# A hybrid decoder block on one core: first attention blocks and first FFN blocks planned ahead, GpSimd's block subtractions split up

## The chip, the cores and the metric

One core of one Trainium2 chip runs the whole layer in one launch. The metric is the device time of that core in microseconds, the median of the runs shown. TensorE (PE) does matrix products and transposes, VectorE (DVE), ScalarE (ACT) and GpSimd (POOL) the rest; SyncE (SP) issues all transfers in order.

## The reference

One layer over 2048 tokens of width 1024, all in float32:

```python
h = rmsnorm(x, g_mix);  p = h @ w_in                        # 1024 -> 2560
y_a = conformer_conv(a_val, a_gate, ...)                    # GLU, causal conv of 31, LayerNorm, swish
y_b = chunked_sgu(b_u, b_v, ...)                            # gelu, LayerNorm, 128x128 mixing per chunk
# stick-breaking attention, 8 heads of 64, 128-query blocks over the causal keys:
z = q @ k.T * d**-0.5;  mask = s_pos < t_pos
log_1m_beta = where(mask, -softplus(z), 0);  log_beta = -softplus(-z)
a = where(mask, exp(log_beta + reverse_cumsum(log_1m_beta) - log_1m_beta), 0);  o = a @ v
x = x + (concat(_rms(y_a), _rms(y_b), _rms(y_c)) * g_out) @ w_out
h = rmsnorm(x, g_ffn);  up = causal_dwconv(h @ w_up)        # 1024 -> 2 x 2816, conv of 3
x = x + (silu(gate) * val) @ w_down;  return rmsnorm(x, g_final)
```

## The kernel before, in words

Every float32 product is three TensorE products of rounded parts (`mm3`, L114: high by high, high by low, low by high); the low part of an operand is its float32 value less the rounded one.

**Projections** (L437 to L514), two halves of 1024 tokens. Key parts `kh_d`, `kl_d`, query parts, values `v_d` and the two other branches' outputs go to DRAM. The convolution runs on VectorE, a step at a time between projection blocks. PSUM has eight banks: `tp` (x transposes) and `cvp` (convolution) lie on the left, `bt` (branch transposes, `pst`) and `pj` (three projection blocks) on the right. The last value blocks leave PSUM through `vs` (L499).

**Attention** (L879 to L923): 320 steps of one 128-query block by up to 512 keys of one head. Four steps are a unit (one head and key chunk), two units (both heads) a chunk of a pair of heads; a query stretch of 512 has four pairs. In a step `front` (L715) makes the scores `pz` (L732, L735), ACT their sigmoids `om` (L737), VectorE the running product (scan, L740 on the diagonal, L745 elsewhere); six steps later `transpose_a` (L752) transposes `om` into `pat` (L758) and splits it into `ah` and `al`; `al` is made by VectorE (L770) for even blocks and by GpSimd (L767) for odd ones; eight steps later `times_v` adds the products with V in `po` (L779, L780). `finish_pair` (L782) brings `po` out as `ych`. `load_kv` fetches keys and values for pairs after the first into `kv`; for the first pair (`pre`, L541) they are in the x tiles' buffers (`xi`).

**Work let in between.** Output projections are generators (`out_proj`, L646; g=0 branches A and B, g=1 the attention's part) whose matmuls are let in behind the score product of a step (`tc.issue_after`), 1.8 stops a step up to step 32, 0.65 behind. After g=1 a row block of 128 tokens is normed into `h` (L682 to L694) and, two row blocks at a time, `store_blocks` (L615) writes seven blocks of `h` to `hc_d`: three as they are, four as differences, made by GpSimd, and by VectorE for the last query stretch. These are the operands of a seven-product scheme for a 2x2 block product, which the FFN uses. `down_blocks` (L598), called every 20 steps from step 40, does the same for w_down: two loads (`wd0`, `wd1`, one buffer each), four subtractions on GpSimd (L607 to L610), four stores.

**Border.** The last out_proj (query stretch 3, g=1) runs with `up_weights(0)` (L959) between; `stage_first` has put the first four blocks of `h` on the chip. `h_blocks` (L1015) transposes a block into `pth` (L1026), casts it (`thh`, L1031) and subtracts (`thl`, L1032). The tiles for these lie where the last out_proj's weights were; their PSUM banks (`ups`) where `atp` and `otp` were.

**FFN** (L1156 on): seven products for each pair of channel blocks (`prod`), then the down product (`pd`).

**What orders the work.** The program is traced in the order of the code, and a planner gives each engine its order ahead of the run: by a simulated time line it takes, of the instructions whose inputs and buffers are ready, the one traced first; `tc.high_priority(offset=n)` counts an instruction as traced n earlier. Each engine then works strictly in that order. A tile waits only for the tiles that had its bytes before (`reuse_waits="tile"`).

Of the kernel before, what the change touches and what calls it, by code (L numbers as in the profile page):

```python
# [15 lines left out]
P = 128  # L16
# [4 lines left out]
def kernel(  # L21
# [114 lines left out]
    xp = pool(cl, "xp", 4)  # L136
    tp = pool(cl, "tp", 2, space=PSUM)
    cvp = pool(cl, "cvp", 1, space=PSUM)
    hp = pool(cr, "hp", 2, "right")
    wp = pool(cr, "wp", 5, "right")  # L140
    rp = pool(cr, "rp", 2, "right")
# [294 lines left out]

    for hf in range(2):  # L437
# [31 lines left out]
        for c0, hd, ld in ((1536, kh_d, kl_d), (1024, qh_d, ql_d)):  # L469
            w = load_w(c0)  # L470
            for ct in range(NPAIR):
# [43 lines left out]
    def load_q(tiles, qs, pr):  # L515
        qA, qB = tiles
        t_s = slice(qs * 512, (qs + 1) * 512)
        dma32(qA[0:64], qh_d[pr, 0:64, t_s])
        dma32(qA[64:128], ql_d[pr, 0:64, t_s])
        dma32(qB[0:64], ql_d[pr, 64:128, t_s])  # L520
        dma32(qB[64:128], qh_d[pr, 64:128, t_s])
        return tiles

    def load_kv(tiles, kc, pr):
        kA, kB, lA, lB, vv = tiles
        k_s = slice(kc * 512, (kc + 1) * 512)
        for hd, th_, tl_ in ((0, kA, lA), (1, kB, lB)):
            hr = slice(64 * hd, 64 * hd + 64)
            for r in (slice(0, 64), slice(64, 128)):
                dma32(th_[r], kh_d[pr, hr, k_s])  # L530
                dma32(tl_[r], kl_d[pr, hr, k_s])
        dma32(
            vv,
            v_d[kc * 4 : kc * 4 + 4, :, pr * 256 : (pr + 1) * 256].rearrange(
                "n p c -> p n c"
            ),
        )
        return tiles


    pre = [  # L541
        xp.tile([P, D], F32R, tag="xi", name=f"pre{i}").rearrange("p (a c) -> p a c", a=2)
        for i in range(4)
    ]
    first_q = load_q((pre[0][:, 0, :], pre[0][:, 1, :]), 0, 0)
    first_kv = load_kv(
        (
            pre[1][:, 0, :], pre[1][:, 1, :], pre[2][:, 0, :], pre[2][:, 1, :],
            pre[3].rearrange("p a (n c) -> p (a n) c", c=256),
        ),  # L550
        0, 0,
    )
    while later:
# [5 lines left out]
    kv = pool(cr, "kv", 2, "right")  # L559
    ap_ = pool(cr, "ap", 1, "right")  # L560
    tp2 = pool(cr, "tp2", 3, "right")
    co = ExitStack()
    opp = pool(co, "opp", 2, "right", space=PSUM)
    zp = pool(cr, "zp", 2, "right", space=PSUM)
    cl.close()
    cl = ExitStack()
    wo = pool(cl, "wo", 1)
# [3 lines left out]
    atp = pool(cl, "atp", 2, space=PSUM)  # L571
    otp = pool(cl, "otp", 2, space=PSUM)
# [3 lines left out]
    G.memset(mask[:, : 512 - P], 0.0)  # L576
    G.memset(mask[:, 512 - P :], 1.0)
    G.affine_select(
        out=mask[:, 512 - P :], in_=mask[:, 512 - P :], pattern=[[1, P]],
        compare_op=ALU.is_ge, fill=0.0, base=0, channel_multiplier=-1,  # L580
    )
# [64 lines left out]
    def out_proj(qs, g, kept=()):  # L646
# [6 lines left out]
        for j in range(4):  # L653
            n = qs * 4 + j
            x1, (yh, yl) = nxt, ys.pop(0)
            for nh in range(2):
# [58 lines left out]
    def front(p, kc, hd, j):  # L715
# [20 lines left out]
        om = ap_.tile([P, 512], F32, tag="om", name="om", bufs=13)[:, :w_]  # L736
# [15 lines left out]
    def transpose_a(p, kc, hd, b, a4):  # L752
# [10 lines left out]
        if b % 2:  # L763
# [3 lines left out]
            G.tensor_tensor(al[:, c_], ar[:, c_], ah[:, c_], op=ALU.subtract)  # L767
# [541 lines left out]
```

## Time and profile before

| | us |
|---|---|
| median of 3 runs (2558.9 to 2566.23) | 2563.68 |
| the profiled execution | 2561.74 |
| its span, first to last instruction | 2559.7 |
| TensorE busy | 2408.8 (94%) |
| VectorE busy | 1852.8 (72%) |
| ACT busy | 1202.3 (47%) |
| GpSimd busy | 1215.6 (47%) |

The mean granted clock of TensorE is 0.976 of full speed. In the views a name such as `al` is the tile written, "<-" the tiles read, L767 the line; "[7.52 <-ACT vs L499]" says that the engine was idle 7.52 us before, until that instruction. SPq is the queue of SP.

### The profile page before, as it was taken

What the parts mean: (1) busy time and instruction counts of PE and PEld (TensorE: products, weight loads), DVE (VectorE), ACT (ScalarE), POOL (GpSimd) and SP (SyncE); (2) the same over time, 40 slices, a digit from 0 to 9 for tenths busy, and PEclk for the clock granted to TensorE, in tenths of its full rate; (3) what the DMA queues carried; (4) which work ended last, traced back from release to release, by engine and by line L of the source; (5) the groups of instructions that cost most, each with busy time, mean ns of one, the idle gap of its engine ahead of it and who ended that gap; (6) DMA issues with size and microseconds to landing.
All of it is one profiled execution on the core that took longest, in us unless ns stands there. A gap on an engine that the chain in (4) does not pass through costs nothing.

```text
span 2559.7 us, 33192 instructions
## 1 busy us (share of the span) xinstructions
PE 2408.8 (94%) x11139; PEld 1962.5 (77%) x11139; DVE 1852.8 (72%) x2360; ACT 1202.3 (47%) x2130; POOL 1215.6 (47%) x929
## 2 busy tenths in 40 slices
PE   7999999968899889998799999999989999999998
PEld 5878778756777678776588888888867888888887
DVE  3881595357798789986588888875558888888555
ACT  4333522365576667773434434454344344345542
POOL 2433552454457454656244444565424444447551
PEclk9999999979999999998999999999989999999999
DMA  4245625399999998876233333497652333337962
GB/s 138 85 146 171 192 83 156 129 260 271 280 295 284 250 270 237 235 216 218 91 104 103 103 103 103 122 335 223 175 181 79 100 106 103 100 107 226 301 186 98
DMA packets 418233, 445.67 MB, mean 174 GB/s; under 512 B 23922, under 2 KB 301694, under 8 KB 418063
## 3 DMA queue, kind: packets, MB, share of 16 engines
q1 hardware_dynamic: 418063, 443.55, 58.3%
q8 instruction: 89, 1.46, 0.3%
q14 instruction: 81, 0.66, 0.1%
HBM read 305.57 MB, written 137.89 MB: 173 GB/s over the span
## 4 chain that ended last, share of the span: by engine, by line
PE 75%; DMA 10%; DVE 6%; issue 3%; POOL 3%; ACT 2%; SPq 1%; POOLq 0%; DVEq 0%; ACTq 0%
PE prod L117 11%; PE prod L116 11%; PE prod L115 11%; PE pd L117 5%; PE pd L116 5%; PE pd L115 5%; PE pjt L115 3%; PE pjt L116 3%; PE pjt L117 3%; PE pat L758 2%; PE pz L732 1%; PE pjd L115 1%; PE pjd L116 1%; PE pjd L117 1%; PE po L780 1%
## 5 line engine op out<-in xcount | busy, mean ns | idle before, releaser
L121 POOL TENSOR_TENSOR wl<-raw,wh 128x512 fp32r<-128x512 f32 (+1 forms) x260 | 381.8, 1470 | 553.7 <-ACT wh L120 543.8
L115 PE MATMUL prod<-thh,wh 128*128 128x512 f32 x1232 | 481.3, 391 | 11.4 <-DVE thl L1032 11.3
L117 PE MATMUL prod<-thh,wl 128*128 128x512 f32 x1232 | 487.0, 395 | 0.0
L116 PE MATMUL prod<-thl,wh 128*128 128x512 f32 x1232 | 485.4, 394 | 0.0
L120 ACT CAST wh<-raw 128x512 fp32r<-128x512 f32 (+1 forms) x260 | 177.4, 684 | 307.6 <-PE prod L116 176.3
L121 POOL TENSOR_TENSOR dwl<-raw,dwh 128x512 fp32r<-128x512 f32 x154 | 222.6, 1476 | 134.5 <-ACT dwh L120 101.8
L115 PEld LDWEIGHTS prod<-thh,wh 128*128 128x128 f32 x1232 | 232.7, 189 | 65.6 <-DVE thl L1032 13.6
L767 POOL TENSOR_TENSOR al<-ar,ah 128x512 fp32r<-128x512 f32 (+2 forms) x160 | 181.9, 1140 | 195.7 <-ACT ah L766 164.9
L116 PEld LDWEIGHTS prod<-thl,wh 128*128 128x128 f32 x1232 | 232.7, 189 | 53.6
L117 PEld LDWEIGHTS prod<-thh,wl 128*128 128x128 f32 x1232 | 232.9, 189 | 46.5
L745 DVE TENSOR_TENSOR_SCAN om<-om,pz 128x512 f32<-128x512 f32 x192 | 239.6, 1269 | 27.6 <-ACT om L737 27.0
L117 PE MATMUL pd<-dwh,sal 128*128 128x512 f32 x616 | 242.5, 394 | 0.0
L116 PE MATMUL pd<-dwl,sah 128*128 128x512 f32 x616 | 241.5, 392 | 0.0
L115 PE MATMUL pd<-dwh,sah 128*128 128x512 f32 x616 | 239.5, 389 | 1.3 <-DVE thl L1032 1.2
L1150 DVE TENSOR_TENSOR sal<-ar,sah 128x512 fp32r<-128x512 f32 x168 | 150.7, 909 | 120.1 <-ACT sah L1149 109.2
L1090 DVE SCALAR_TENSOR_TENSOR cv<-u,vec,cv 128x1024 f32<-128x1024 f32 x176 | 222.6, 1287 | 13.7 <-ACT cv L1088 12.0
L737 ACT ACTIVATE om<-pz 128x512 f32<-128x512 f32 (+2 forms) x320 | 168.4, 544 | 90.6 <-PE pz L735 87.3
L1037 DVE TENSOR_TENSOR u<-prod,u 128x512 f32<-128x512 f32 x220 | 147.2, 686 | 66.4 <-PE prod L117 63.4
L758 PE MATMUL pat<-ident,om 128*128 128x128 f32 x1088 | 178.2, 279 | 5.0 <-DVE al L770 1.2
L758 PEld LDWEIGHTS pat<-ident,om 128*128 128x128 f32 x1088 | 138.2, 144 | 41.1 <-DVE al L770 5.2
L121 POOL TENSOR_TENSOR wl<-s,wh 128x512 fp32r<-128x512 f32 x88 | 121.7, 1383 | 97.9 <-ACT wh L120 93.4
L1149 ACT CAST sah<-ar 128x512 fp32r<-128x512 f32 x168 | 97.2, 583 | 148.6 <-PE pd L116 103.0
(278 smaller groups left out, 5205.8 us busy)
## 6 DMA issues: line engine op xcount, KB each, us to landing
raw<-in_w_up_dram SPq DMA_DIRECT2D x88, 512.0 KB
ar<-s_d SPq DMA_DIRECT2D x112, 256.0 KB
s_d<-act SPq DMA_DIRECT2D x110, 256.0 KB
raw<-in_w_in_dram SPq DMA_DIRECT2D x40, 512.0 KB
raw<-wd_d SPq DMA_DIRECT2D x40, 512.0 KB
vv<-v_d SPq DMA_DIRECT2D x39, 512.0 KB
x_d<-x SPq DMA_DIRECT2D x32, 512.0 KB
raw<-in_w_down_dram SPq DMA_DIRECT2D x30, 512.0 KB
```

The costliest lines, as they stand in the source:

```text
L115: T.matmul(ps, lh, rh, start=start, stop=False)
L116: T.matmul(ps, lh, rl, start=False, stop=False)
L117: T.matmul(ps, ll, rh, start=False, stop=stop)
L120: A.copy(hi, src)
L121: G.tensor_tensor(lo, src, hi, op=ALU.subtract)
L737: A.activation(om, pz[:, :w_], AF.Sigmoid, scale=-0.125)
L745: V.tensor_tensor_scan(om[:, ::-1], om[:, ::-1], pz[:, ::-1], initial=p.carry[hd, j], op0=ALU.mult, op1=ALU.bypass,)
L758: T.transpose(pt[:, j * P : (j + 1) * P], a4[j][:, b * P : (b + 1) * P], ident)
L767: G.tensor_tensor(al[:, c_], ar[:, c_], ah[:, c_], op=ALU.subtract)
L1037: V.tensor_tensor(dst, ps, other, op=ALU.add)
L1090: V.scalar_tensor_tensor(cv, u[:, j : j + HALF], cw(j), cv, op0=ALU.mult, op1=ALU.add)
L1150: V.tensor_tensor(lo, ar, hi, op=ALU.subtract)
```

## The change

It has six parts. (1) Pools: `rp`, `xp`, `wp`, `hp` are stacked anew on the right, so that the attention's `ap` (mask and `om`) lies where the raw weights and x tiles were; the score and transpose banks (`zp`, `atp`) take the left banks of `tp` and `cvp`, `otp` and `opp` the right ones of `bt` and `pj`. (2) The first pair's queries, keys and values are loaded into the `uv` buffers of branch B, traced ahead of the last query projection; the mask and the first eight `front` calls have their priority raised by 250. `om` has 12 buffers for 13. (3) `down_blocks` stops behind its loads and behind each operation, is called every 5 steps for 20, and writes its fourth difference into `b11` and not into a tile of its own. (4) `store_blocks` writes one difference into a new tile `t2`, stores each block behind its operation, and stops behind each on GpSimd; the norm's multiplication by `gffn_b` is in two halves with stops; the rate of stops behind step 32 is 0.9 for 0.65. GpSimd's `al` has its priority raised by 150. (5) In the last out_proj the squares go to PSUM in two halves. (6) `h_blocks` raises the first two blocks of the first half by 120. `load_q` and `load_kv` only move up.

```diff
--- before.py
+++ after.py
@@ -133,12 +133,13 @@
     sp = pool(cl, "sp", 4)
-    xp = pool(cl, "xp", 4)
     tp = pool(cl, "tp", 2, space=PSUM)
     cvp = pool(cl, "cvp", 1, space=PSUM)
+    rp = pool(cr, "rp", 2, "right")
+    xp = pool(cr, "xp", 4, "right")
+    wp = pool(cr, "wp", 5, "right")
     hp = pool(cr, "hp", 2, "right")
-    wp = pool(cr, "wp", 5, "right")
-    rp = pool(cr, "rp", 2, "right")
     bt = pool(cr, "bt", 1, "right", space=PSUM)
@@ -434,6 +435,31 @@
         dma32(v_d[n], vt.rearrange("p a b d -> p (a b d)"))
+    def load_q(tiles, qs, pr):
@@ -468,6 +494,21 @@
             w = load_w(c0)
+            if hf == 1 and c0 == 1024:
+                pre = [
+                    bp.tile([P, 4, 512], F32R, tag="uv", name=f"pre{i}", bufs=2)
+                    for i in range(2)
+                ]
+                first_q = load_q((pre[0][:, 0, :], pre[0][:, 1, :]), 0, 0)
+                first_kv = load_kv(
+                    (
+                        pre[0][:, 2, :], pre[0][:, 3, :], pre[1][:, 0, :],
+                        pre[1][:, 1, :],
+                        pre[1][:, 2:4, :].rearrange("p a (n c) -> p (a n) c", c=256),
+                    ),
+                    0, 0,
+                )
             for ct in range(NPAIR):
@@ -512,73 +553,38 @@
             hT = nxt
-    def load_q(tiles, qs, pr):
...
-    pre = [
-        xp.tile([P, D], F32R, tag="xi", name=f"pre{i}").rearrange("p (a c) -> p a c", a=2)
...
     while later:
...
     cr = ExitStack()
-    kv = pool(cr, "kv", 2, "right")
+    AHEAD, AHEAD_STEPS = 250, 8
     ap_ = pool(cr, "ap", 1, "right")
     tp2 = pool(cr, "tp2", 3, "right")
+    kv = pool(cr, "kv", 2, "right")
     co = ExitStack()
+    otp = pool(co, "otp", 2, "right", space=PSUM)
     opp = pool(co, "opp", 2, "right", space=PSUM)
-    zp = pool(cr, "zp", 2, "right", space=PSUM)
     cl.close()
     cl = ExitStack()
+    zp = pool(cr, "zp", 2, space=PSUM)
+    atp = pool(cr, "atp", 2, space=PSUM)
     wo = pool(cl, "wo", 1)
...
     xo = pool(cl, "xo", 2)
-    atp = pool(cl, "atp", 2, space=PSUM)
-    otp = pool(cl, "otp", 2, space=PSUM)
     mask = ap_.tile([P, 512], F32, tag="mask", name="mask")
-    G.memset(mask[:, : 512 - P], 0.0)
-    G.memset(mask[:, 512 - P :], 1.0)
-    G.affine_select(
-        out=mask[:, 512 - P :], in_=mask[:, 512 - P :], pattern=[[1, P]],
-        compare_op=ALU.is_ge, fill=0.0, base=0, channel_multiplier=-1,
-    )
+    with tc.high_priority(offset=AHEAD):
+        G.memset(mask[:, : 512 - P], 0.0)
+        G.memset(mask[:, 512 - P :], 1.0)
+        G.affine_select(
+            out=mask[:, 512 - P :], in_=mask[:, 512 - P :], pattern=[[1, P]],
+            compare_op=ALU.is_ge, fill=0.0, base=0, channel_multiplier=-1,
+        )
     ch = ExitStack()
@@ -603,14 +609,15 @@
             b11, b12, b21, b22 = r0[:, 0:512], r0[:, 512:D], r1[:, 0:512], r1[:, 512:D]
-            t3 = xo.tile([P, 512], F32, tag="t3", name="wd3", bufs=1)
-            G.tensor_tensor(t3, b22, b12, op=ALU.subtract)
-            G.tensor_tensor(b12, b12, b11, op=ALU.subtract)
-            G.tensor_tensor(b22, b22, b12, op=ALU.subtract)
-            G.tensor_tensor(b21, b21, b22, op=ALU.subtract)
-            for i, t_ in enumerate((b12, b22, t3, b21)):
+            yield
+            for i, t_, u_, v_ in (
+                (0, b12, b12, b11), (1, b22, b22, b12), (3, b21, b21, b22),
+                (2, b11, b22, b11),
+            ):
+                G.tensor_tensor(t_, u_, v_, op=ALU.subtract)
                 nc.sync.dma_start(wd_d[i, :, f, :], t_)
-            yield
+                yield
     def store_blocks(n, he, ho, eng):
@@ -620,15 +627,17 @@
         nc.sync.dma_start(dst[2], b22)
+        t2 = xo.tile([P, 512], F32, tag="t2", name="t2", bufs=1)
         t3 = xo.tile([P, 512], F32, tag="t3", name="t3", bufs=1)
-        eng.tensor_tensor(t3, b22, b12, op=ALU.subtract)
-        eng.tensor_tensor(b12, b12, b11, op=ALU.subtract)
-        eng.tensor_tensor(b22, b22, b12, op=ALU.subtract)
-        eng.tensor_tensor(b21, b21, b22, op=ALU.subtract)
-        nc.sync.dma_start(dst[3], b22)
-        nc.sync.dma_start(dst[4], t3)
-        nc.sync.dma_start(dst[5], b12)
-        nc.sync.dma_start(dst[6], b21)
+        for i, t_, u_, v_ in (
+            (4, t3, b22, b12), (5, b12, b12, b11), (3, t2, b22, b12), (6, b21, b21, t2),
+        ):
+            eng.tensor_tensor(t_, u_, v_, op=ALU.subtract)
+            nc.sync.dma_start(dst[i], t_)
+            if eng is G:
+                yield
     def load_y(n, g, kept):
@@ -680,22 +689,41 @@
                     h = xo.tile([P, D], F32, tag="h", name="h")
-                    ms = yb_.tile([P, 1], F32, tag="ms", name="ms2")
-                    A.activation(h, x1, AF.Square, scale=1.0 / 32.0, accum_out=ms)
+                    ms = yb_.tile([P, 2], F32, tag="ms", name="ms2")
                     tm = yb_.tile([P, 1], F32, tag="tm", name="tm2")
                     r = yb_.tile([P, 1], F32, tag="r", name="r_ffn")
-                    rstd(r, ms, tm)
+                    if qs == NQ - 1:
+                        for c in range(2):
+                            jk = otp.tile([P, 512], F32, tag="otp", name="jk2")
+                            A.activation(
+                                jk, x1[:, c * 512 : (c + 1) * 512], AF.Square,
+                                scale=1.0 / 32.0, accum_out=ms[:, c : c + 1],
+                            )
+                        V.tensor_scalar(
+                            tm, ms[:, 0:1], ms[:, 1:2], EPS, op0=ALU.add, op1=ALU.add
+                        )
+                        G.tensor_tensor(r, tm, mhalf[:, :1], op=ALU.pow)
+                    else:
+                        A.activation(
+                            h, x1, AF.Square, scale=1.0 / 32.0, accum_out=ms[:, 0:1]
+                        )
+                        rstd(r, ms[:, 0:1], tm)
                     if qs == NQ - 1:
...
                     else:
+                        yield
                         G.tensor_scalar(h, x1, r, 1.0, op0=ALU.mult, op1=ALU.mult)
-                        G.tensor_tensor(h, h, gffn_b, op=ALU.mult)
+                        yield
+                        for c in (slice(0, 512), slice(512, D)):
+                            G.tensor_tensor(h[:, c], h[:, c], gffn_b[:, c], op=ALU.mult)
+                            yield
                     if j % 2 == 0:
...
                     else:
-                        store_blocks(n, even, h, V if qs == NQ - 1 else G)
+                        yield from store_blocks(n, even, h, V if qs == NQ - 1 else G)
                 yield
@@ -733,7 +761,7 @@
         T.matmul(pz[:, :w_], qt[:, j_s], lt[:, :w_], start=False, stop=True)
-        om = ap_.tile([P, 512], F32, tag="om", name="om", bufs=13)[:, :w_]
+        om = ap_.tile([P, 512], F32, tag="om", name="om", bufs=12)[:, :w_]
         A.activation(om, pz[:, :w_], AF.Sigmoid, scale=-0.125)
@@ -764,7 +792,8 @@
             A.copy(ah[:, c_], pt[:, c_])
-            G.tensor_tensor(al[:, c_], ar[:, c_], ah[:, c_], op=ALU.subtract)
+            with tc.high_priority(offset=150):
+                G.tensor_tensor(al[:, c_], ar[:, c_], ah[:, c_], op=ALU.subtract)
         else:
@@ -869,7 +898,7 @@
     WO_0, WO_S = 2, 3
-    FILL_0, RATE_0, RATE = 14, 1.8, 0.65
+    FILL_0, RATE_0, RATE = 14, 1.8, 0.9
     NU = len(units)
@@ -882,14 +911,18 @@
                 pairs[qs, pr] = Pair(qs, pr)
-            a4s.setdefault(u, []).append(front(pairs[qs, pr], kc, hd, j))
+            if s_ < AHEAD_STEPS:
+                with tc.high_priority(offset=AHEAD):
+                    a4s.setdefault(u, []).append(front(pairs[qs, pr], kc, hd, j))
+            else:
+                a4s.setdefault(u, []).append(front(pairs[qs, pr], kc, hd, j))
             if s_ == 0:
...
                 load_wo((s_ - WO_0) // WO_S)
-        if s_ >= 40 and s_ % 20 == 0:
+        if s_ >= 40 and s_ % 5 == 0:
             next(wd_gen, None)
@@ -921,7 +954,7 @@
                     rms_at[s_ + 3] = qs
-    for gen in ready:
+    for gen in [wd_gen] + ready:
         for _ in gen:
@@ -1012,25 +1045,27 @@
         return th[i].tile([P, 512], F32R, tag="t", name=nm)
+    def h_parts(hf, b, st, k):
+        pt = bank("pth")
+        for j in range(4):
+            T.transpose(pt[:, j * P : (j + 1) * P], st[j][:, k * P : (k + 1) * P], ident)
+        side = int(b >= 4) if hf == 0 else int(b < 3)
+        hi, lo = t_tile(side, "thh"), t_tile(side, "thl")
+        A.copy(hi, pt)
+        V.tensor_tensor(lo, pt, hi, op=ALU.subtract)
+        return hi, lo
     def h_blocks(hf, first=()):
...
                 staged.append(stage_h(hf, len(staged), len(staged) < 5))
-            st = staged[b]
             parts = []
-            for k in range(KH):
-                pt = bank("pth")
-                for j in range(4):
-                    T.transpose(
-                        pt[:, j * P : (j + 1) * P], st[j][:, k * P : (k + 1) * P], ident
-                    )
-                side = int(b >= 4) if hf == 0 else int(b < 3)
-                hi, lo = t_tile(side, "thh"), t_tile(side, "thl")
-                A.copy(hi, pt)
-                V.tensor_tensor(lo, pt, hi, op=ALU.subtract)
-                parts.append((hi, lo))
+            with tc.high_priority(offset=120) if hf == 0 and b < 2 else nullcontext():
+                for k in range(KH):
+                    parts.append(h_parts(hf, b, staged[b], k))
             yield parts
```

## Rows read from the trace of the kernel before

**Rows 1.** Table by stage: length; busy PE, PEld, DVE, ACT, POOL; clock, DMA share, GB/s.

```profile
0.00:500.00 500.00, 474.22 (x2157) 388.92 (x2158) 281.77 (x389) 171.54 (x277) 198.96 (x134) 0.99 0.43 138
500.00:532.00 32.00, 16.74 (x70) 12.47 (x69) 21.04 (x34) 13.84 (x34) 15.81 (x18) 0.74 0.63 203
532.00:700.00 168.00, 140.55 (x697) 111.67 (x696) 117.28 (x148) 95.93 (x212) 79.67 (x68) 0.93 1.04 271
700.00:950.00 250.00, 223.99 (x1191) 182.38 (x1188) 211.60 (x238) 165.97 (x346) 141.49 (x119) 0.96 0.95 274
950.00:1172.00 222.00, 212.07 (x1140) 172.48 (x1141) 196.06 (x214) 159.16 (x315) 120.11 (x97) 0.99 0.78 221
1172.00:1268.00 96.00, 69.07 (x314) 52.91 (x314) 55.09 (x81) 35.76 (x66) 39.64 (x32) 0.88 0.54 180
1268.00:2560.00 1292.00, 1272.19 (x5579) 1041.66 (x5577) 970.00 (x1261) 560.11 (x884) 619.92 (x464) 0.99 0.48 147
```

**Rows 2.** TensorE's waits, 500 to 1290: for what, us in total, times, longest.

```profile
PE po L780 <- POOL al L767: 26.8, 12, 7.4
...
PE pz L732 <- DVE om L745: 14.6, 23, 2.5
...
PE prod L115 <- DVE thl L1032: 10.0, 3, 9.2
...
PE pz L732 <- ACT vs L499: 7.5, 1, 7.5
```

**Rows 3.** Time line at the attention's start: start, us, engine, line, operation, [idle before, releaser].

```profile
508.08 0.39 PE L117 MATMUL pjd<-wh,hTl 128*128 128x512 f32 x1
...
518.82 0.47 PE L732 MATMUL pz<-pre,pre 128*128 128x128 f32 x1 [7.52 <-ACT vs L499]
...
521.47 0.44 SPq L91 DMA_DIRECT2D lA<-kl_d  x1
...
529.10 0.79 PE L779 MATMUL po<-ah,pre 128*128 128x512 f32 x1 [0.44 <-ACT ah L769]
```

**Rows 4.** Table by stage, the same start after its gap.

```profile
518.80:532.00 13.20, 8.83 (x34) 6.86 (x35) 8.99 (x10) 6.31 (x15) 6.79 (x7) 0.63 0.75 232
```

**Rows 5.** The tile `pre`: the last of its loads, duration ns, first and last start.

```profile
L91 SPq DMA_DIRECT2D pre<-v_d x1: 490/490/490, 307.7 to 307.7; - x1
```

**Rows 6.** Groups by line, 500 to 1290; count, busy us, mean ns, idle before, releasers.

```profile
L740 DVE TENSOR_TENSOR_SCAN om<-om,mask 128x128 f32<-128x128 f32 (+3 forms) x128 | 136.2, 1093 | 25.7 <-ACT om L737 25.3
...
L767 POOL TENSOR_TENSOR al<-ar,ah 128x512 fp32r<-128x512 f32 (+2 forms) x160 | 181.9, 1140 | 195.7 <-ACT ah L766 164.9 <-PE pz L735 17.9 <-PE pz L732 5.0
...
L694 POOL TENSOR_TENSOR h<-h,gffn_b 128x1024 f32<-128x1024 f32 x12 | 29.1, 2428 | 0.4
...
L1032 DVE TENSOR_TENSOR thl<-pth,thh 128x512 fp32r<-128x512 f32 x28 | 18.6, 686 | 14.9 <-ACT thh L1031 14.9
```

**Rows 7.** Time line of GpSimd and TensorE at an in-place wait.

```profile
766.62 1.27 POOL L626 TENSOR_TENSOR h<-h 128x512 f32<-128x512 f32 x1 [6.40 <-DMA kB<-kh_d]
...
770.51 0.50 PE L780 MATMUL po<-al,vv 128*128 128x512 f32 x1 [3.60 <-POOL al L767]
```

**Rows 8.** Time line of GpSimd at a late load.

```profile
843.77 1.26 POOL L607 TENSOR_TENSOR wd<-wd,wd 128x512 f32<-128x512 f32 x1 [9.87 <-DMA wd<-in_w_down_dram]
```

**Rows 9.** SP's waits, 595 to 960.

```profile
SPq L612 <- POOL wd L607: 15.5, 5, 4.4
```

**Rows 10.** Time lines of TensorE and VectorE at the border to the FFN.

```profile
1179.38 0.50 PE L780 MATMUL po<-al,vv 128*128 128x512 f32 x1 [3.41 <-POOL al L767]
...
1216.57 0.39 PE L117 MATMUL pab<-woh,ycl 128*128 128x512 f32 x1
...
1218.52 1.29 DVE L689 SCALAR_TENSOR_TENSOR h<-x,r_ffn,gffn_b 128x1024 f32<-128x1024 f32 x1 [0.72 <-POOL r_ffn L112]
...
1224.82 0.69 DVE L627 TENSOR_TENSOR h<-h 128x512 f32<-128x512 f32 x1
...
1226.17 0.79 PE L115 MATMUL prod<-thh,wh 128*128 128x512 f32 x1 [9.21 <-DVE thl L1032]
```

More of the change, by code (lines that the diff above doesn't have):

```diff
@@ L1 @@
-from contextlib import ExitStack
+from contextlib import ExitStack, nullcontext
 import concourse.bass as bass
@@ L435, in v_steps, with load_kv @@
         dma32(v_d[n], vt.rearrange("p a b d -> p (a b d)"))
+    def load_q(tiles, qs, pr):
+        qA, qB = tiles
+        t_s = slice(qs * 512, (qs + 1) * 512)
+        dma32(qA[0:64], qh_d[pr, 0:64, t_s])
+        dma32(qA[64:128], ql_d[pr, 0:64, t_s])
+        dma32(qB[0:64], ql_d[pr, 64:128, t_s])
+        dma32(qB[64:128], qh_d[pr, 64:128, t_s])
+        return tiles
+    def load_kv(tiles, kc, pr):
+        kA, kB, lA, lB, vv = tiles
+        k_s = slice(kc * 512, (kc + 1) * 512)
+        for hd, th_, tl_ in ((0, kA, lA), (1, kB, lB)):
+            hr = slice(64 * hd, 64 * hd + 64)
+            for r in (slice(0, 64), slice(64, 128)):
+                dma32(th_[r], kh_d[pr, hr, k_s])
+                dma32(tl_[r], kl_d[pr, hr, k_s])
+        dma32(
+            vv,
+            v_d[kc * 4 : kc * 4 + 4, :, pr * 256 : (pr + 1) * 256].rearrange(
+                "n p c -> p n c"
+            ),
+        )
+        return tiles
     for hf in range(2):
@@ L470 @@
             w = load_w(c0)
+            if hf == 1 and c0 == 1024:
[9 more added lines that the diff above has]
+                        pre[1][:, 2:4, :].rearrange("p a (n c) -> p (a n) c", c=256),
+                    ),
+                    0, 0,
+                )
             for ct in range(NPAIR):
@@ L514 @@
             hT = nxt
-    def load_q(tiles, qs, pr):
[L516 to L536, printed above, removed]
-        )
-        return tiles
-    pre = [
-        xp.tile([P, D], F32R, tag="xi", name=f"pre{i}").rearrange("p (a c) -> p a c", a=2)
[L543 to L551, printed above, removed]
-    )
     while later:
@@ L570 @@
     xo = pool(cl, "xo", 2)
-    atp = pool(cl, "atp", 2, space=PSUM)
-    otp = pool(cl, "otp", 2, space=PSUM)
     mask = ap_.tile([P, 512], F32, tag="mask", name="mask")
-    G.memset(mask[:, : 512 - P], 0.0)
-    G.memset(mask[:, 512 - P :], 1.0)
-    G.affine_select(
-        out=mask[:, 512 - P :], in_=mask[:, 512 - P :], pattern=[[1, P]],
-        compare_op=ALU.is_ge, fill=0.0, base=0, channel_multiplier=-1,
-    )
+    with tc.high_priority(offset=AHEAD):
[5 more added lines that the diff above has]
+        )
     ch = ExitStack()
@@ L682, in out_proj @@
                     h = xo.tile([P, D], F32, tag="h", name="h")
-                    ms = yb_.tile([P, 1], F32, tag="ms", name="ms2")
-                    A.activation(h, x1, AF.Square, scale=1.0 / 32.0, accum_out=ms)
+                    ms = yb_.tile([P, 2], F32, tag="ms", name="ms2")
                     tm = yb_.tile([P, 1], F32, tag="tm", name="tm2")
                     r = yb_.tile([P, 1], F32, tag="r", name="r_ffn")
-                    rstd(r, ms, tm)
+                    if qs == NQ - 1:
[12 more added lines that the diff above has]
+                            h, x1, AF.Square, scale=1.0 / 32.0, accum_out=ms[:, 0:1]
+                        )
+                        rstd(r, ms[:, 0:1], tm)
                     if qs == NQ - 1:
@@ L1020, in h_blocks @@
                 staged.append(stage_h(hf, len(staged), len(staged) < 5))
-            st = staged[b]
             parts = []
-            for k in range(KH):
-                pt = bank("pth")
-                for j in range(4):
-                    T.transpose(
-                        pt[:, j * P : (j + 1) * P], st[j][:, k * P : (k + 1) * P], ident
-                    )
-                side = int(b >= 4) if hf == 0 else int(b < 3)
-                hi, lo = t_tile(side, "thh"), t_tile(side, "thl")
-                A.copy(hi, pt)
-                V.tensor_tensor(lo, pt, hi, op=ALU.subtract)
-                parts.append((hi, lo))
+            with tc.high_priority(offset=120) if hf == 0 and b < 2 else nullcontext():
+                for k in range(KH):
+                    parts.append(h_parts(hf, b, staged[b], k))
             yield parts
```

## The prediction

> **What bounds the kernel now.** First the table by stage: its first figure behind each stretch is TensorE's busy time. TensorE is busy 2408.8 of 2559.7 us, and where it is not lies mostly in the middle [rows 1]: the projections lose 26 us in 500, the FFN 20 us in 1292, but the attention and its two borders (500 to 1268) lose 105.6 of 768, 15.3 in the first 32 us and 26.9 in the last 96. The granted clock falls there too: 0.74 and 0.88 at the borders, 0.93 and 0.96 in the first two thirds of the attention, 0.99 behind. The DMA share is 1.04 and 0.95 in those two thirds, so the transfer engines are full there; VectorE is busy 211.6 of 250 us in the second. Next the list of TensorE's waits from 500 to 1290 [rows 2]: the longest is 26.8 us in 12 times of the product with V (L780) for `al`, which GpSimd makes; then scans (`om`), one wait of 10 us for `thl` and one of 7.5 us for `vs`. Then the time line around each. The profiled execution took 2561.7 us (span 2559.7 and 2.0 around it), 1.9 below the median of the runs, 2563.7; I sum against the first and add 1.9 at the end.
>
> **Start of the attention.** The last projection product starts at 508.08 and ends about 508.5; the first score product starts at 518.82, because its PSUM bank was the projections' and `vs` left it late [rows 3]. [...] The change puts the score banks where the convolution's and the x transposes' were, done long before, and lets the first 8 scores and scans (all of pair 0) run up to 250 instructions early. Their inputs were never late: `pre` was loaded by 307.7 us [rows 5], and in the new place (the `uv` buffers, free after SGU's tail) it can be loaded beside the last query projection. Moving it costs 13 issues on SP and 2 MB, about 7.5 us at the 271 GB/s of the full stretch [rows 1], in a stage whose DMA share is 0.43: hidden; without that cover at most 7.5 us, below nothing no way, as nothing waited for it. The moved scans are some 8.7 us of VectorE (8 of 1.093 [rows 6]), in a stage where it is busy 282 of 500: hidden. What is late next: `po` now takes the banks of `pst` and of the projections, so the first V product still waits for the last `vs` (the one of 518.82 at the worst, against 529.10), and pair 1's scores wait for their loads, of which `lA` goes out at 521.47 [rows 3] and can't be used much before 524 to 526, against 528.13. Both ends: 0 (pair 1's loads set everything) and 19 us (9.7 idle, 4.4 idle behind it, 4.9 of half clock). I take 8, nearest to what lies between 521 and 529.
>
> **GpSimd's queue.** It works in order, so an `al` stands behind whatever was planned ahead of it. Of the 26.8 us, 3.4 fall in the end border. Two kinds make up the other 23.4. One: ready or self-made waits. At 766.62 `h` L626, written in place, waits 6.40 us until a transfer that reads the same block has landed, and the `al` behind it costs TensorE 3.60 us [rows 7]; four `wd` operations in a row at 660 to 666 cost 1.8 in the same way. With a tile `t2` of its own, priority for `al` and pieces of at most 1.3 us, these go: 7 us with their smaller like. Two: L607 waits for the load of w_down itself, 9.87 us at 843.77 [rows 8], and TensorE 7.4 us behind it, the longest of [rows 2]; with three like it (2.5, 2.4 and 1.6) 14 us. The `yield` between load and first operation puts that operation five steps (about 10 us) lower in priority, but the planner issues what is ready in its own clock: `pre`, last in the program, was loaded 200 us early. So I count a third of the 14, 5 us. Together 12; ends 0 (order by readiness changes nothing) and 23.4. Added: `h` times `gffn_b` in two halves of 1.29 us for one of 2.43, 12 times, 2 us, on an engine busy half the time: hidden; if not, 2 us. Keeping 12 instead of 13 `om` buffers still leaves three steps between the last reader and the next writer; the trace names no `om` buffer wait, and I cost it at 0 (at most 3 us).
>
> [...]
>
> **Rates.** The fill rate goes from 0.65 to 0.9, as a g=1 output projection now has 56 stops for 32: all of them take 291 of 300 instead of 219 of 228, so as much is left at the end. But a g=0 one keeps its 32 stops and runs faster: between steps 32 and 67 nine stops more of 0.19 MB (x, y and x1 tiles, 1.5 MB in 8 stops) are 1.7 MB, 6 us at 271 GB/s where the DMA share is 1.04, given back later where it is 0.78 [rows 1]. Ends 0 and 6 lost; I take 2.
>
> **End border.** TensorE starts the last `pab` matmul at 1216.57 and the first FFN product at 1226.17, since VectorE does the norms of two row blocks and four block subtractions (1218.52 to 1225.51) ahead of `thl` [rows 10]. With blocks 0 and 1 120 instructions ahead, the first subtraction (0.686 us [rows 6]) and a cast, taken as long, give a product at about 1218.2; the norms' 7 us move behind them, beside the first two products (24 matmuls, 5.5 us at the 0.23 from start to start that the full clock shows) and their transposes, which hide about as much: of 8 us I keep 6.5. The first products ran at the lower level (0.79 us for 0.39 [rows 10]): 1. The `al` at 1179.38, 3.41 us behind a whole 2.4 us `h`, becomes 1.3: 2. A wait of 4.3 us before the first block's transposes goes too (their banks no longer wait for `po`), but TensorE needs the last pair's `ych` right behind all the same: 0. The squares into PSUM take ACT 0.3 us more each: hidden, ACT is busy 36 of 96; their wait for `h` passes to VectorE, where it would cost 2 us. Sum 9.5; ends 0 and 20 (9.2, 4.3, 3.4 and 3 of lower clock).
>
> **Sum:** 8 + 12 + 9.5 - 2 = 27.5; 2561.7 - 27.5 = 2534.2, and 1.9 to the median: 2536.
>
> **Rivals.** (a) All these stalls go, each term at its far end: 19 + 23.4 + 20 is 62, 2501. For it: the clock of 0.93 and 0.96 from 532 to 950 [rows 1], of which I count nothing (0.07 of 168 and 0.04 of 250 us are 22). Against: the full DMA engines. (b) The transfers hide it: from 532 to 950 the share is 0.95 to 1.04, so what starts earlier waits for its `kA` or `wd`; only the end border's 9.5 less 2 stays: 2556. Against: no transfer stands among TensorE's longest waits [rows 2]. (c) SP becomes the bound, slower: with an `al` let in ahead of each `wd` operation, each of an f block's last three stores waits one `al` (1.14 us) longer: 3.4 us in 11 blocks, 38 us of SP, and behind it stand the key loads. It decides once these are later than their eight-step lead; if half comes through it is 19, and as much waiting again arises where the refill of `wd0` now follows its last store at once (2 us in 11 blocks, 22): 41 against the 27.5, 2563.7 + 13 = 2577. (d) The priorities move nothing, since readiness orders the queues: only the 7 us of the in-place waits stay: 2557.
>
> **How the numbers follow.** Mine 0.50, (a) 0.18, (b) 0.13, (c) 0.12, (d) 0.07. Under 0.3% (7.7 us) this kernel's measurements can't tell a change from none; that bound lies at 2556, on which (b) and (d) fall: half of their 0.20 is no change. So faster 0.78, same 0.10, slower 0.12. Mine alone runs from 2518 to 2552, by the ends of its terms. For 8 in 10 I reach to (a) and, above, past (b) and (d): 2498 to 2562.
>
> **What would show it.** Right: score products before 508; a gap there of a few us; the `al` waits at a third or half of 26.8; the first FFN product within 2 us of the last `pab`; the clock above 0.95 from 532 on. Wrong: `kA`, `kB` or `lA` among TensorE's longest waits (b or c), SP's wait for `wd` well above 15.5 (c), or L607 waits of 5 to 10 us still in GpSimd's list with `al` behind them.

## The result and the profile after

The changed kernel takes **2578.09 us** (median of 4 runs, 2575.63 to 2581.32) against 2562.76 for the kernel before on the same chip: ratio 1.0061, 95% interval 1.0042 to 1.0079, so some 15.6 us slower where 27.5 us faster was forecast. Its profiled execution took 2580.27 us (span 2578.2).

The table by stage, at about the same events as in [rows 1]; columns as there:

```profile
0.00:500.00 500.00, 471.79 (x2144) 386.12 (x2145) 280.64 (x388) 169.30 (x270) 197.97 (x133) 0.98 0.43 137
500.00:532.00 32.00, 21.10 (x88) 15.12 (x86) 20.89 (x36) 15.55 (x43) 14.47 (x15) 0.83 0.61 188
532.00:700.00 168.00, 139.69 (x686) 114.65 (x687) 113.66 (x141) 89.69 (x197) 77.52 (x67) 0.89 1.01 279
700.00:950.00 250.00, 214.87 (x1117) 174.86 (x1116) 212.81 (x223) 155.70 (x323) 147.38 (x123) 0.94 0.92 266
950.00:1195.00 245.00, 227.22 (x1220) 181.73 (x1218) 218.04 (x235) 175.74 (x353) 135.56 (x110) 0.99 0.75 211
1195.00:1290.00 95.00, 69.42 (x324) 52.26 (x324) 55.45 (x83) 38.08 (x74) 37.66 (x31) 0.89 0.54 176
1290.00:2578.00 1288.00, 1270.28 (x5571) 1040.03 (x5569) 968.66 (x1259) 559.66 (x883) 621.16 (x464) 0.99 0.48 147
```

TensorE does 4.4 us more in the first 32 us than before, and 9.1 less from 700 to 950, while VectorE and GpSimd are busier there (212.8 for 211.6, 147.4 for 141.5). The transfer engines have become emptier, not fuller (0.92 for 0.95). The last score product comes 24 us later (1190.9 for 1166.5).

TensorE's waits, 500 to 1310 (for what, us in total, times, longest), against [rows 2]:

```profile
PE pz L760 <- DVE om L773: 22.2, 23, 9.6
PE po L809 <- POOL al L796: 20.2, 12, 5.0
PE pat L786 <- DVE al L799: 15.2, 15, 2.9
PE pz L760 <- DMA kA<-kh_d: 14.9, 4, 5.9
PE prod L115 <- DVE thl L1055: 10.8, 3, 10.1
```

The wait for GpSimd's `al` fell by 6.6 us, that for `vs` is gone, that for `thl` is the same. Three grew: scans by 7.6 us, less than the one wait of 9.6 among them; VectorE's own `al` (15.2 us here as `pat`'s wait for 1.2 before; with `po`'s waits for it, which fell, 15.7 for 7.9); and `kA`, which was not among the longest. Two of the three are waits for VectorE. Its groups by form give a clue. First three widths of the diagonal scan and `ycl` in the kernel before, 500 to 1290 (count, busy us, mean ns, idle before, releasers), and then the changed kernel, 380 to 1290:

```profile
L740 DVE TENSOR_TENSOR_SCAN om<-om,mask 128x512 f32<-128x512 f32 x32 | 43.9, 1371 | 2.8 <-ACT om L737 2.7
L740 DVE TENSOR_TENSOR_SCAN om<-om,mask 128x384 f32<-128x384 f32 x32 | 38.2, 1193 | 5.2 <-ACT om L737 5.1
L740 DVE TENSOR_TENSOR_SCAN om<-om,mask 128x256 f32<-128x256 f32 x32 | 36.9, 1153 | 6.1 <-ACT om L737 6.0
L801 DVE SCALAR_TENSOR_TENSOR ycl<-yp,vec,ych 128x512 fp32r<-128x512 f32 x16 | 14.3, 896 | 5.6 <-ACT ych L800 3.0 <-DMA yl_d<-ycl 2.6
```

```profile
L768 DVE TENSOR_TENSOR_SCAN om<-om,mask 128x512 f32<-128x512 f32 x32 | 50.1, 1566 | 1.9 <-ACT om L765 1.9
L768 DVE TENSOR_TENSOR_SCAN om<-om,mask 128x384 f32<-128x384 f32 x32 | 43.9, 1373 | 11.6 <-ACT om L765 11.4
L768 DVE TENSOR_TENSOR_SCAN om<-om,mask 128x256 f32<-128x256 f32 x32 | 31.2, 977 | 3.1 <-ACT om L765 3.1
L830 DVE SCALAR_TENSOR_TENSOR ycl<-yp,vec,ych 128x512 fp32r<-128x512 f32 x16 | 22.2, 1387 | 8.3 <-ACT ych L829 8.3
```

Three of these groups take 6 to 8 us longer for the same work, and the scan of 128x256 takes 5.7 us less; that of 128x128 takes 2.1 us more. With all four widths the 128 diagonal scans take 148.2 us for 139.9. The scan of the other blocks, whose second operand lies in PSUM, takes 1269 ns for 1269 and VectorE's `al`, which reads PSUM too, 673 for 673. So of these groups only the ones with two operands in SBUF changed their length, though not all in the same direction. The largest case, as a time line of the changed kernel:

```profile
737.13 1.01 POOL L796 TENSOR_TENSOR al<-ar,ah 128x384 fp32r<-128x384 f32 x1
738.01 9.67 DVE L830 SCALAR_TENSOR_TENSOR ycl<-yp,vec,ych 128x512 fp32r<-128x512 f32 x1
738.09 1.29 POOL L618 TENSOR_TENSOR wd<-wd 128x512 f32<-128x512 f32 x1
739.33 1.29 POOL L637 TENSOR_TENSOR h<-h 128x512 f32<-128x512 f32 x1
...
744.63 1.28 POOL L618 TENSOR_TENSOR wd<-wd 128x512 f32<-128x512 f32 x1
745.85 1.28 POOL L618 TENSOR_TENSOR wd<-wd,wd 128x512 f32<-128x512 f32 x1
749.53 0.69 PE L760 MATMUL pz<-kA,qA 128*128 128x384 f32 x1 [9.57 <-DVE om L773]
```

`ycl`, 0.9 us in the mean before, stands on VectorE for 9.67 us while GpSimd runs eight operations from 738.09 to 747.13 without a gap, and ends 0.55 us after the last. Behind it VectorE's scans wait, and TensorE for these 9.57 us. It is one hold in the one execution that was profiled, and it makes up the whole growth of `ycl`: without it the other 15 take 12.5 us, 0.84 us in the mean.

### The profile page after: what moved, and what is told of

It reads as the page before. It is cut to its first block, busy times and chain, and to the rows that moved or that the text cites. A ratio compares the mean times of both kernels' runs of the same rounds, so it can differ in the third digit from the quotient of the medians.

```text
span 2578.2 us, 33258 instructions
## 1 busy us (share of the span) xinstructions
PE 2414.4 (94%) x11139; PEld 1964.8 (76%) x11139; DVE 1870.2 (73%) x2360; ACT 1203.7 (47%) x2138; POOL 1231.7 (48%) x941
## 4 chain that ended last, share of the span: by engine, by line
PE 74%; DMA 9%; DVE 6%; POOL 4%; issue 3%; ACT 3%; SPq 1%; DVEq 0%; POOLq 0%; ACTq 0%
PE prod L115 11%; PE prod L117 11%; PE prod L116 11%; PE pd L117 5%; PE pd L115 5%; PE pd L116 5%; PE pjt L115 3%; PE pjt L117 3%; PE pjt L116 3%; PE pat L786 3%; PE pz L760 2%; PE pab L115 1%; PE pab L116 1%; PE pab L117 1%; PE po L809 1%
## 5 line engine op out<-in xcount | busy, mean ns | idle before, releaser
L773 DVE TENSOR_TENSOR_SCAN om<-om,pz 128x512 f32<-128x512 f32 x192 | 239.5, 1269 | 29.5 <-ACT om L765 28.5
L786 PE MATMUL pat<-ident,om 128*128 128x128 f32 x1088 | 180.2, 285 | 17.7 <-DVE al L799 15.2
L786 PEld LDWEIGHTS pat<-ident,om 128*128 128x128 f32 x1088 | 139.1, 146 | 55.3 <-DVE al L799 24.5
L768 DVE TENSOR_TENSOR_SCAN om<-om,mask 128x128 f32<-128x128 f32 (+3 forms) x128 | 144.7, 1159 | 32.7 <-ACT om L765 32.3
```

Of the source, the lines that this page charges most:

```text
L773: V.tensor_tensor_scan(om[:, ::-1], om[:, ::-1], pz[:, ::-1], initial=p.carry[hd, j], op0=ALU.mult, op1=ALU.bypass,)
L786: T.transpose(pt[:, j * P : (j + 1) * P], a4[j][:, b * P : (b + 1) * P], ident)
```

## The experiments

Two theories went into them. **Port theory** (a name only, no run shows a port): a VectorE instruction with two operands in SBUF and a GpSimd instruction hold each other up, and the change, which puts GpSimd's work in denser runs, makes more of it. The second half of that is seen only in part: GpSimd's runs of 3 us and more without a gap (of 0.06 us) between 500 and 1290 sum to 281 us in the kernel before and to 314 in s2_pool, but to 285 in the changed kernel and 277 in s7_wd. **Transfer theory**: what is loaded or stored earlier crowds the transfers. Ratios are to the kernel before, run beside each group of them (2560.9 to 2561.9 us); 0.001 is 2.6 us.

**s1_start** (the start alone: score banks, first scores 250 instructions ahead, `pre` loaded in the projections)

```
-    pre = [xp.tile(...)] ... ; front(...)
+    (in the last projection) pre = [bp.tile(..., tag="uv")] ...
+    with tc.high_priority(offset=250): front(...)   # first 8 steps
```

> The kernel before with parts (1) and (2) alone: new pool places, first pair loaded beside the last query projection, mask and first eight fronts 250 ahead, 12 om buffers. Port theory (VectorE's instructions with two SBUF operands are held while GpSimd runs without a gap, and the change's GpSimd parts make longer runs): this part is innocent, 2555 to 2563, step 32 some 5 us earlier as in the changed kernel, no VectorE instruction of 128x512 above 4 us. Transfer theory (earlier loads and faster fill crowd the transfers): 2566 to 2572, kA among TensorE's longest waits and the gain of step 32 lost again by step 112.

Measured 2564.95, ratio 1.0009 (0.9993 to 1.0025): nothing that shows. The expectation's "step 32 some 5 us earlier" comes out (4.0 us), but the step before it is 9.7 us later and the one behind it 2.6, so there is no lead to lose; TensorE waits 5.72 and 5.29 us for `kA` ahead of it. In the profiled execution (2567.52 us) the gap before the first FFN product is 14.7 us for 9.6, since the squares start only when a store of `h` has landed (ACT idle 13.61 us before them, 8.12 in the kernel before), though this part edits nothing there. So what the start costs by itself is not separated from that.

**s2_pool** (GpSimd's parts alone: priority for `al`, one operation at a time, `t2`, halves, rate 0.9, 12 `om` buffers)

```
+    with tc.high_priority(offset=150): G.tensor_tensor(al, ...)
+    for i, t_, u_, v_ in (...): G.tensor_tensor(t_, u_, v_, ...); dma_start(...); yield
-    RATE = 0.65
+    RATE = 0.9
```

> The kernel before with parts (3) and (4) alone (and 12 om buffers, as the new tile needs the space): w_down blocks stop behind each operation and every 5 steps, al 150 ahead, t2, halves, stops, rate 0.9. Port theory: the loss sits here, 2572 to 2590, with ycl or diagonal scans on VectorE stretched to several us beside unbroken GpSimd runs, and VectorE's busy time 10 to 20 us above that of before. Transfer theory: 2563 to 2570, VectorE's busy time as before. My forecast's own mechanism (waits for al gone): 2550.

Measured 2573.08, ratio 1.0045 (1.0028 to 1.0061): 11.5 us of the loss, without the start. Its diagonal scans take 148.2 us, as in the whole change, and VectorE is busy 11.7 us more than before, as the port theory has it. But neither is stretched to several us, which it also forecast: the longest diagonal scan takes 2.25 us (2.81 before) and the longest `ycl` 1.80 (1.80 before).

**s3_border** (the end border alone: squares into PSUM, blocks 0 and 1 at priority 120)

```
+    with tc.high_priority(offset=120): parts.append(h_parts(...))   # b < 2
```

> The kernel before with parts (5) and (6) alone: squares of the last out_proj into PSUM in halves, first two h blocks 120 ahead. Forecast's mechanism: first FFN product within 2 us of the last pab, 2554 to 2558. What the changed kernel's trace shows (a gap of 10.13 us before the first FFN product all the same): no gain, 2560 to 2566.

Measured 2557.48, ratio 0.9987 (0.9972 to 1.0002): 3.3 us faster at the most likely, just within the error. The gap from the last `pab` to the first FFN product is 9.1 us for 9.6, so what little came is not from that gap.

**s4_rate** (the fill rate alone: `RATE = 0.9`)

> The kernel before with the fill rate of 0.9 for 0.65 and nothing else: the output projections run ahead and are done some 70 steps early. Transfer theory: the early part suffers, 2572 or more, kB, kA or vv waits of TensorE longer than the 2.8 us of before. Port theory: TensorE's fill alone is harmless, 2558 to 2568, unless GpSimd's block work, which it pulls forward and packs closer, meets VectorE more often: then VectorE's busy time rises and the time with it.

Measured 2566.74, ratio 1.0020 (1.0004 to 1.0036): 5.1 us slower. The diagonal scans take 145.1 us.

**p1_scan** and **p2_pool_scan** (one edit on the kernel before, and on s2_pool): on diagonal blocks the sigmoid stays in PSUM, and the scan reads it there, one operand in SBUF for two.

```
-        A.activation(om, pz[:, :w_], AF.Sigmoid, scale=-0.125)
+        sg = pz[:, :w_] if diag else om
+        A.activation(sg, pz[:, :w_], AF.Sigmoid, scale=-0.125)
...
-                om[:, ::-1], om[:, ::-1], mask[...]
+                om[:, ::-1], sg[:, ::-1], mask[...]
```

> The kernel before, with one thing changed: on diagonal blocks the sigmoid is written in place into its PSUM bank and the scan reads it there, so that this scan has one operand in SBUF (the mask) and not two. Port theory: these 121 scans, 132.4 us in all from 532 to 1172 in the kernel before (1376, 1194, 1162 and 637 ns by width), all fall to the same length for each width whatever GpSimd does, at about the 1268 ns that the PSUM scan of 512 takes and less in proportion for the narrower ones, some 105 us in all; VectorE's busy time falls by about 25 us, and the time falls by a few us where TensorE waits for scans (`om`): 2552 to 2560. Transfer theory: the scans may get shorter, the time stays within 3 us of before, 2561.

> GpSimd's parts of the change (as in s2_pool: 2573.1, 11.7 above before) with the same edit of the diagonal scans. Port theory: s2_pool's 142 us of diagonal scans fall to the same 105 us, and most of the loss of 11.7 us goes: 2555 to 2564. Transfer theory: the loss stays, 2569 to 2575, since the loads and stores are issued as in s2_pool.

Measured: p1_scan 2558.43, ratio 0.9986 (0.9974 to 0.9999); p2_pool_scan 2555.04, ratio 0.9978 (0.9965 to 0.9990). The edit is worth 3.6 us on the kernel before and **17 us on GpSimd's parts**, which turns their loss of 11.5 us into a gain of 5.6. Loads and stores of s2_pool are all still there, and the time that the transfer theory forecast (2569 to 2575) did not come. One thing is not held fixed: the planner orders the program anew, and about a tenth of each engine's instructions (189 of SP's 1501 issues) stand in another order than in s2_pool. What that is worth was not tried by itself. s2_pool and p2_pool_scan, VectorE and GpSimd, 500 to 1290:

```profile
L747 DVE TENSOR_TENSOR_SCAN om<-om,mask 128x512 f32<-128x512 f32 x32 | 47.6, 1486 | 5.6 <-ACT om L744 5.6
L775 POOL TENSOR_TENSOR al<-ar,ah 128x512 fp32r<-128x512 f32 x96 | 132.6, 1384 | 134.0 <-ACT ah L773 98.4 <-PE pab L116 10.6 <-PE pab L117 9.5
L631 POOL TENSOR_TENSOR t<-h 128x512 f32<-128x512 f32 x12 | 20.3, 1694 | 0.0
```

```profile
L748 DVE TENSOR_TENSOR_SCAN om<-pz,mask 128x512 f32<-128x512 f32 x32 | 38.6, 1207 | 1.3 <-ACT pz L745 0.9
L776 POOL TENSOR_TENSOR al<-ar,ah 128x512 fp32r<-128x512 f32 x96 | 123.8, 1291 | 143.5 <-ACT ah L774 126.8 <-PE pab L116 13.0 <-PE pab L117 2.0
L631 POOL TENSOR_TENSOR t<-h 128x512 f32<-128x512 f32 x12 | 15.9, 1325 | 0.0
```

Both sides were held: GpSimd's `al` was 1384 ns and is 1291, `t<-h` 1694 and 1325. The edit makes a scan no shorter by itself: the shortest single ones of each width, 128 to 512, were 0.39, 0.65, 0.92 and 1.19 us with two operands in SBUF (kernel before) and are the same in p2_pool_scan. What goes is the spread: the longest ones were 1.45, 1.97, 2.02 and 2.25 us in s2_pool and are 0.43, 0.69, 0.96 and 1.22. All 128 together take 104.1 us for 148.2. TensorE's waits for VectorE's `al` fall from 18.7 us to 1.8, and its waits for scans rise from 15.0 to 24.5, so the waits by name explain 7 us of the 17. All of TensorE's idle time falls by 12.9 us between the two profiled executions, and its busy time by 5.4.

**s5_al** (priority 150 for `al` alone)

> The kernel before with the priority of 150 for GpSimd's `al` alone. Forecast's mechanism: `al` goes ahead of `wd` and of h times gffn_b, a gain of some 3 to 7 us. Port theory: no more GpSimd work than before and no longer pieces without a gap, so no loss: 2555 to 2562. Transfer theory: no transfer moves, no change: 2561.

Measured 2562.84, ratio 1.0004 (0.9994 to 1.0014): no change. The late load's wait is still the longest (6.84 us for 7.4).

**s6_blocks** and **s7_wd** (the two other halves of s2_pool: the `h` blocks with the rate; the w_down blocks)

```
+ s6:  t2 = xo.tile(...); yield from store_blocks(...); two halves of h * gffn_b; RATE = 0.9; om bufs=12
+ s7:  for i, t_, u_, v_ in (...): G.tensor_tensor(...); dma_start(...); yield    # down_blocks
```

> The kernel before with the h blocks' part alone: tile t2, halves of h times gffn_b, one operation at a time, fill rate 0.9, 12 om buffers; `wd` and `al` as before. Port theory: GpSimd's short operations follow each other in runs of their own, diagonal scans grow by part of s2_pool's 10 us: 2565 to 2570. Transfer theory: the rate alone gave 5.4 us, and the w_down loads and stores as before give nothing more: about 2567. Then s2_pool's other 6 us are wd's.

> The kernel before with the w_down blocks' part alone: one operation at a time, stores behind each, the last one in place. Since `al` alone gave nothing (2562.8 against 2561.9), and the h blocks' part gave 7.7 of the 11.7 us of s2_pool, what is left for this part is about 4 us: 2564 to 2567, with diagonal scans a few us above before's 132.4. Forecast's mechanism: 3 to 7 us faster, 2555 to 2559. Transfer theory: wd0's earlier refill and the stores between keep SP longer, 2565 or more, with key loads among TensorE's waits.

Measured: s6_blocks 2569.55, ratio 1.0034 (1.0021 to 1.0047); s7_wd 2569.61, ratio 1.0025 (1.0006 to 1.0044), with 143.5 and 149.3 us of diagonal scans. Each loses by itself; the sum of the two (15.1 us) is above s2_pool's 11.5, within the intervals. s7_wd's size is loose: its times lie in two groups, 2559 to 2562 and 2568 to 2574. Its profiled execution, with the 149.3 us, took 2559.54, no longer than the kernel before. So a larger sum of scan times alone does not make a kernel slower.

**p3_after_scan** (the whole change with p1_scan's edit)

> The whole change with the sigmoid of diagonal blocks in PSUM and their scan reading it there. Port theory: it gives back what the same edit gave on top of s2_pool (18 us): 2558 to 2563, the diagonal scans at 1.21, 0.95, 0.67 and 0.41 us by width, and no wait of 9 us for a scan. `ycl` and `sq` still have two operands in SBUF, so one long `ycl` may remain. Transfer theory: the early start and the fuller transfers keep the loss: 2573 or more.

Measured 2561.07, ratio 0.9994 (0.9980 to 1.0008). The same edit is worth 17 us here as well. The loss against the kernel before is gone with the 128 scans' second SBUF operand, but not the 2 us that p1_scan is better still; `ycl` (1027 ns) stays above its 896.

**p4_rate_scan** (rate 0.9 and p1_scan's edit on the kernel before)

> The kernel before with the fill rate of 0.9 (alone 5.4 us slower) and the diagonal scans from PSUM (alone 3.5 us faster). Port theory: the rate costs because GpSimd's norms and block work stand closer together, and goes with the scans' second SBUF operand: 2556 to 2560. Transfer theory: it costs because x, y and x1 tiles come while the transfers are full, and stays: 2563 to 2565.

Measured 2562.27, ratio 0.9996 (0.9982 to 1.0011). The rate costs 5.1 us alone and, against p1_scan, 2.6 with the edit. These are too near for a verdict: part of it is likely the scans' second SBUF operand, and 2 to 3 us, the forecast's own figure, may be transfers.

**c3_all** (p2_pool_scan and s3_border's part)

> The change without its early start (GpSimd's parts and the end border's) with the diagonal scans from PSUM. If the parts add up: p2_pool_scan's 2555.0 less the 3.9 of the border's part is 2551, which beats both kernels. If the border's gain was only another order of the projections in s3_border, it stays at 2555.

Measured 2558.03, ratio 0.9982 (0.9969 to 0.9996): the border's part adds nothing that shows, though the gap before the first FFN product is 7.8 us for p2_pool_scan's 9.3.

**e6_last_subs** and **e7_subs_border** (p2_pool_scan and c3_all, with the block subtractions of the last two row blocks on GpSimd)

```
-    yield from store_blocks(n, even, h, V if qs == NQ - 1 else G)
+    yield from store_blocks(n, even, h, V if qs == NQ - 1 and j == 1 else G)
```

> p2_pool_scan with the block subtractions of the last two row blocks on GpSimd, which is idle there, in place of VectorE. If these four (0.69 us each from start to start 0.72, 2.9 us) are what stands ahead of `thl`, the gap from the last `pab` to the first FFN product falls from 9.3 to about 6.5 us and the time by 2.9: 2552. If `thl` waits for the last norms (whose x1, gffn_b and r_ffn lie where the first `thl` and `thh` tiles come to lie) by itself or for a transfer, the gap stays above 8.5 and the time at 2555.

> c3_all (GpSimd's parts, the end border's part and the diagonal scans from PSUM: 2558.0) with the same four subtractions on GpSimd. If the border's part then works as the forecast had it (first product after one cast and one subtraction), the gap falls below 5 us: 2553. If the norms hold it, as in e6_last_subs, 2555.

Measured: e6_last_subs 2556.97, ratio 0.9976 (0.9965 to 0.9988), gap 6.8 us for p2_pool_scan's 9.3; e7_subs_border **2553.12, ratio 0.9970 (0.9959 to 0.9982)**, gap 5.2 for c3_all's 7.8, faster than both kernels, though not clear of p2_pool_scan and e6_last_subs. The subtractions did stand ahead of `thl`: 2.5 of their 2.9 us went from the gap, both times. In e6 the time doesn't show it (its ratio is p2_pool_scan's), so only the gap is shown there. The border of the changed kernel, and then of e7_subs_border:

```profile
1237.37 0.39 PE L117 MATMUL pab<-woh,ycl 128*128 128x512 f32 x1
...
1239.86 0.57 ACT L1054 CAST thh<-pth 128x512 fp32r<-128x512 f32 x1
1240.90 1.28 DVE L713 SCALAR_TENSOR_TENSOR h<-x,r_ffn,gffn_b 128x1024 f32<-128x1024 f32 x1 [1.76 <-DMA hc_d<-h]
...
1244.36 0.69 DVE L637 TENSOR_TENSOR t<-h 128x512 f32<-128x512 f32 x1
...
1247.14 2.48 DVE L1055 TENSOR_TENSOR thl<-pth,thh 128x512 fp32r<-128x512 f32 x4
1247.88 0.80 PE L115 MATMUL prod<-thh,wh 128*128 128x512 f32 x1 [10.13 <-DVE thl L1055]
```

```profile
1218.68 0.39 PE L117 MATMUL pab<-woh,ycl 128*128 128x512 f32 x1
...
1221.64 1.28 DVE L707 SCALAR_TENSOR_TENSOR h<-x,r_ffn,gffn_b 128x1024 f32<-128x1024 f32 x1 [0.72 <-POOL r_ffn L700]
1223.16 2.49 DVE L1046 TENSOR_TENSOR thl<-pth,thh 128x512 fp32r<-128x512 f32 x4 [0.23 <-DMA x_d<-x]
1223.91 0.51 PE L115 MATMUL prod<-thh,wh 128*128 128x512 f32 x1 [1.65 <-DVE thl L1046]
```

The cast of the first block is done at 1240.43, but `thl` comes last on VectorE all the same, behind two norms and four subtractions. In the program's allocation its tile lies on the last row block's `x1` and the second `thh` on `gffn_b`, which the last norm reads until 1244.3 (the second cast starts at 1244.35, 3.93 us after its engine fell idle). The priority of 120 did not pass that. In e7_subs_border `thl` still waits 0.23 us for the store that reads this `x`.

## Why the prediction was wrong

**GpSimd's queue** is the step that failed, by an effect that it left out. It counted 12 us saved, and GpSimd's added pieces and the moved scans as "hidden", since each engine had idle time. Measured: 11.5 us lost, and some 2 gained (p2_pool_scan against p1_scan, within the error) once the scans hold no second operand in SBUF. Busy shares don't show that two engines hold each other up: in the kernel before, the diagonal scan of 512 took 1371 ns in the mean where its shortest was 1190, and [rows 6] gave a mean over four widths, in which this can't be seen. The form view would have shown it ahead of the change, and an instruction with two SBUF operands held beside GpSimd's list was a rival that the prediction did not have; its slower one, (c), did not come: SP's wait for `wd` is 15.2 us (595 to 960), with [rows 9] 15.5, so that its 2577 lies next to the measured 2578 is chance.

The runs show the hold in both directions: from s2_pool to p2_pool_scan VectorE's scan of 512 falls from 1486 to 1207 ns in the mean and GpSimd's `al` of 512 from 1384 to 1291. How long a hold lasts they show in one case only. Held by one operation at a time, `ycl` would have waited for at most one of GpSimd's, about 1.3 us; it stood beside eight, 9.67 us, while none of these took more than 1.29 us. So there the engine that had work queued without a gap went on and the other stayed out.

Of the step's own terms: the in-place waits went and `al`'s wait fell from 26.8 to 20.2, a quarter and not a half. The late-load waits stayed, as the prediction's "wrong if" has it: `wd` waits 7.33 us at 847.23 (put down to the load of `lB`, and not to that of `wd`) and TensorE 5.01 behind it at 852.58. The 1.8 us at 660 to 666, which the prediction counts among the ready ones, stand behind a load too: the first of those four `wd` waits 3.80 us for it at 660.40. s5_al says the priority alone is worth nothing that shows.

**Start of the attention** (8 us): its lower end, 0. Scores did start ahead of 508 (406.75), but that gave no lead: pair 1's first score product starts at 529.80 for 528.13, that of step 16 at 548.80 for 544.40 and that of step 31 at 588.96 for 579.92; step 32 alone is 4.7 us earlier (589.97 for 594.68), and step 33 is 2.0 later again. Pair 1's first load goes out 3.8 us behind the last projection product, at 515.33 as at 511.83 before. In the program's allocation `qA`, `qB`, `kA` and `kB` lie where that projection's operand `hTl` was, and SP stands for 5.2 us on a store of `yh` ahead of the load; which of the two sets its time is not shown. What was gained became waits for `kA` (3.46, 5.92 and 5.28 us at 529.80, 548.80 and 575.17). SP's wait from 507 to 516, and two of TensorE's:

```profile
SPq L91 <- ACT yh L324: 5.2, 1, 5.2
```

```profile
529.80 0.76 PE L760 MATMUL pz<-kA,qA 128*128 128x128 f32 x2 [3.46 <-DMA kA<-kh_d]
...
548.80 0.77 PE L760 MATMUL pz<-kA,qA 128*128 128x128 f32 x2 [5.92 <-DMA kA<-kh_d]
```

The granted clock from 532 to 700 fell to 0.89 from 0.93, where over 0.95 was looked for. No run shows the 4.9 us of half clock in this step's upper end; from 518.8 to 532 the clock was 0.71 for the 0.63 of [rows 4], and no time came of it. Rival (b) is right for this part alone.

**Rates** (2 us lost): 5.1 alone, 2.6 without the scans' second operand: so the 2 us are not contradicted, but 2.6 is not clear of noise, and that the rest goes with that operand is likely and not shown.

**End border** (9.5 us): 0 in the whole change; the gap is 10.5 us for 9.6. Its step "blocks 0 and 1 ahead, the norms move behind them" failed, since order on VectorE was set by the buffers and what was ready, as rival (d) has it for priorities. Nor did the 1 us for the first products' clock come: the first takes 0.80 us for 0.79. The `al` term, 2, isn't separately shown.

Alone, the three parts cost 2.3 + 11.5 - 3.3 = 10.5 us, and the whole 15.6. The single wait of 9.6 us stands only in the whole change's profiled execution. That it makes up the 5 us between is likely but not shown: the intervals are some 4 us wide each way.

## What to carry to other kernels

Before giving GpSimd more work or denser work, list VectorE's instructions by form and compare mean with shortest: those with two SBUF operands that are above it (here 1371 ns for 1190) may already wait for GpSimd. Put one operand in PSUM if the producer can write there; that was an edit of three lines here, worth 3.6 us by itself and 17 on GpSimd's parts, where the whole rescheduling lost 15.6. And a priority moved an instruction here only as far as the buffers of its result let it (in s3_border the gap before the first FFN product stayed 9.1 us for 9.6): look at what lay there before.

## What the runs showed of the hardware

In one case a VectorE instruction with two SBUF operands stood for 9.67 us, 0.9 in the mean before, beside eight GpSimd operations that followed each other within 1.24 us from start to start. And VectorE's time and the kernel's are not exchanged at one rate: the edit freed 36 us of diagonal scans in the kernel before for 3.6 us of time, and 44 us in s2_pool for 17. It is likely that what counts is whether such a hold falls where TensorE waits next; no run tried that by itself.
